# Rotary tables in rows of frequency and half with four whole stores per supertile, a new order for the first head group, and one sum for the output weights' squares

## The chip, the cores and the metric

The kernel runs on one core of a Trainium2 chip. The metric is the time of one execution on the device in microseconds (us); lower is better.

The engines are called as in the profile: PE multiplies matrices, PEld loads its stationary operand, DVE, ACT and POOL do elementwise work, and SP issues nearly all DMAs, one after the other, in the order in which the program hands them to it. "SPq" in a row is the time that SP spends on issuing one DMA. What lands later in SBUF is the transfer itself.

## The reference

Two layers of an encoder over 2048 tokens with 1024 features. Each layer normalises its input, projects it, runs eight heads of banded attention with a learned bias and four heads of retention with rotary phases beside each other, gates both, projects back and adds to its input. What the change touches is the rotary phase:

```python
def rotary_tables(positions, dim):
    inv_freq = 1.0 / (ROPE_BASE ** jnp.linspace(0.0, 1.0, dim // 2, dtype=jnp.float32))
    ang = positions.astype(jnp.float32)[:, None] * inv_freq[None, :]
    return jnp.cos(ang), jnp.sin(ang)

def apply_rotary(t, cos, sin):
    t1, t2 = jnp.split(t, 2, axis=-1)
    return jnp.concatenate([t1 * c - t2 * s, t1 * s + t2 * c], axis=-1)

def hybrid_layer(x, norm_gain, w_in, w_out, rel_bias, cos, sin):
    proj = rms_norm(x, norm_gain) @ w_in
    aq, ak, av, ag, rq, rk, rv, rg = jnp.split(proj, cuts, axis=-1)
    ya = chunked_rel_attention(aq, ak, av, rel_bias)
    yr = chunkwise_retention(rq, rk, rv, cos, sin)
    return x + jnp.concatenate([ya * silu(ag), yr * silu(rg)], -1) @ w_out
```

## The kernel before, in words

**Tiles and stages.** The tokens are cut into 4 supertiles of 512, the heads of a layer into 4 groups of two attention heads and one retention head. For a layer l, a group s and a supertile n the kernel computes: `dense_T` (from L590), four projections transposed (q, k of attention, then q, k of retention, tiles `dT`, matmuls in L763, or in quarters per token tile in L745 for the very first); `dense_V` (from L775), values and gates for the four token tiles of the supertile (tiles `dV`, L783). Each is 24 matmuls of 128x512, since every operand is split into an upper and a lower fp16 part (`hTh`, `hTl` of the input, `whT`, `wlT` of the weights) and three products are taken. The `dT` and `dV` tiles share two PSUM buffers in turn, so a tile starts only when the one before last has been read out.

**Attention and retention** of the supertile are then woven into the dense work of the next one, unit by unit. A unit of attention (its name holds group, supertile, token tile a, head: `pT_0_1_3_0` is group 0, supertile 1, a = 3, head 0) is: scores `S` on PE (L831, L832), `sc` on DVE (L835), exponential `sc` and its upper part `pq` on ACT (L838, L840), the lower part on POOL (L841), a DMA transpose to `pT` issued by SP (L843), and `o` on PE (L853, L854), which waits for `pT`. Retention (L888 on) needs q and k turned by the rotary tables: ACT reads `dT` out (L695), SP loads the halves exchanged (`swp`, L699, L700), POOL multiplies and adds ("the turn", L703 to L705), ACT and DVE split the result (L708, L711, L714), and SP transposes the keys (`kt`, L718). `swp` has one buffer, so the second `swp` of a supertile waits for the first turn.

**The tables.** `tables()` (L83) works out cosine and sine of position times frequency for one or two supertiles with DVE steps (L94 to L107), two Sin on ACT (L118, L119) and a negating copy (L121), stores them to DRAM (`tab`, L127 to L130), and `dense_T` loads them back as `tabc`, `tabs` (L646, L647) for every supertile. ACT's exponential and its Sin need different tables, and each exchange shows as an ACT_TABLE_LOAD. Three generators run: for supertile 0 (one letter `t` in the lists below is one step of it), for 1 and 2 together (`u`) and for 3 (`v`).

**Token tiles.** The input of group 0 is normalised on the fly, token tile by token tile, in steps named by the lists: `xsq` squares (ACT, L256), `xrs` the inverse root (DVE, POOL L219), `xmul` the scaling (DVE, L263), then for tokens 0 to 3 `xtr` transposes on PE (L272) and for 4 to 15 `xdma` DMA transposes (SP, L243 upper, L244 lower) after `xhi` (ACT, L278) and `xlo` (DVE, L286). `W` and `V` steps scale the weight sections of the group (`hi` on ACT L1412, `lo` on DVE L1415).

**What sets the order.** On PE, DVE, ACT and POOL the order is always the program's. In group 0 of layer 0 it is written by hand: the string given to `do()` (L1449) up to the first values, then the table `listed` (L1454), whose pairs of lists are done in turn as the attention units of supertiles 0 to 3 go by. SP keeps program order until the values of supertile 0 are done; from there the framework places most SP instructions by when their data comes, and only those marked keep their program order. `later(k, ...)` puts a store off by k turns of these lists.

**Output weights.** `prep_Omax` (L505) finds the scale of the output weights of a layer from the sum of their squares, 8 sections of 128 rows, adding section by section on DVE.

## Time and profile before

| | us |
|---|---|
| median of 3 runs | 2036.86 |
| lowest and highest of them | 2033.1, 2038.18 |
| profiled execution, its own time | 2034.96 |
| its span in the trace | 2033.0 |
| PE busy in it | 1988.2 (98%) |
| DVE, ACT, POOL busy | 1241.9, 1154.5, 705.8 |

The profiled execution lies 1.9 us below the median, and its time is 2.0 us above its span. PE is busy for nearly all of the span, so a gain must come out of PE's idle time or out of the stretches in which its clock is not at full speed. In the rows of the timelines each line gives start, duration, engine, line and operation, the tiles written and read, a count, and in brackets the idle time of the engine just before with what ended it. The windows' rows give length, then for PE, PEld, DVE, ACT and POOL the busy time with the instructions started, then PE's granted clock, the DMA engines' busy share and GB/s.

### The profile page before, as it was taken

To read this page: it belongs to the slowest core of one execution; us is meant where nothing else is said; L and a number is where in the kernel's file an instruction comes from. 1 tells how busy PE (TensorE), PEld (TensorE's weight loads), DVE (VectorE), ACT (ScalarE), POOL (GpSimd) and SP (SyncE) were. 2 spreads that over 40 slices of the span, in tenths; PEclk is the share of its full clock that TensorE was granted. 3 is DMA by queue.
4 is the path that set the end of the run, shared out by engine and by line. 5 is a ranking of instruction groups with operands and counts; after the bars stand their busy time and mean duration, and the time that the engine had idled before them with its cause. 6 is when DMAs were issued, how large, how long until landed. Compare 5 with 4: busy or idle time off the path is not lost.

```text
span 2033.0 us, 36844 instructions
## 1 busy us (share of the span) xinstructions
PE 1988.2 (98%) x12918; PEld 1046.3 (51%) x12918; DVE 1241.9 (61%) x3676; ACT 1154.5 (57%) x2526; POOL 705.8 (35%) x701
## 2 busy tenths in 40 slices
PE   7998999999999999999999999999999999999998
PEld 5444555555555555554444555555555555555544
DVE  7787766665656655676554556565655566557543
ACT  7566756466666655555445556555656565455432
POOL 1444443443344434420003444344434443443100
PEclk9999999999999999999999999999999999999999
DMA  8788775456585754899874547554656665558874
GB/s 232 184 179 163 171 141 128 104 131 140 124 183 123 164 125 104 175 226 268 220 184 101 120 104 164 113 123 104 161 119 146 160 157 133 120 116 188 229 203 135
DMA packets 645690, 313.47 MB, mean 154 GB/s; under 512 B 459232, under 2 KB 602080, under 8 KB 645504
## 3 DMA queue, kind: packets, MB, share of 16 engines
q1 hardware_dynamic: 645504, 311.12, 66.1%
q8 instruction: 101, 1.65, 0.3%
q14 instruction: 85, 0.70, 0.1%
HBM read 123.26 MB, written 41.98 MB: 81 GB/s over the span
## 4 chain that ended last, share of the span: by engine, by line
PE 86%; DMA 4%; DVE 3%; ACT 2%; POOL 2%; issue 2%; SPq 1%; POOLq 0%; ACTq 0%; DVEq 0%
PE dT L763 29%; PE dV L783 27%; PE dO L1161 15%; PE r L888 4%; PE o L853 3%; PE S L832 3%; PE S L831 3%; DMA pT<-pq 2%; PE o L854 2%; POOL swp L704 0%; PE dT L745 0%; DVE sc L835 0%; DMA xa<-in_x_dram 0%; DMA swp<-rot 0%; ACT stO0m L320 0%
## 5 line engine op out<-in xcount | busy, mean ns | idle before, releaser
L841 POOL TENSOR_TENSOR pq<-sc,pq 128x640 f16<-128x640 f32 (+4 forms) x256 | 322.8, 1261 | 958.0 <-ACT pq L840 497.4
L838 ACT ACTIVATE sc<-sc,mq,cT 128x640 f32<-128x640 f32 (+4 forms) x256 | 218.3, 853 | 416.0 <-DVE mq L837 294.2
L783 PE MATMUL dV<-whV,hTh 128*128 128x512 f16 x1024 | 352.1, 380 | 1.1 <-DVE gt L801 1.1
L783 PE MATMUL dV<-wlV,hTh 128*128 128x512 f16 x1024 | 352.2, 380 | 0.0
L783 PE MATMUL dV<-whV,hTl 128*128 128x512 f16 x1024 | 352.0, 379 | 0.0
L763 PE MATMUL dT<-hTh,whT 128*128 128x512 f16 x1008 | 348.3, 381 | 3.1 <-DMA hTh<-hTl 3.1
L763 PE MATMUL dT<-hTh,wlT 128*128 128x512 f16 x1008 | 348.1, 381 | 0.0
L763 PE MATMUL dT<-hTl,whT 128*128 128x512 f16 x1008 | 346.6, 379 | 0.0
L783 PEld LDWEIGHTS <-hTh 128*128 128x128 f16 x2048 | 196.3, 98 | 214.8 <-DVE gt L801 2.6
L763 PEld LDWEIGHTS <-whT 128*128 128x128 f16 x2016 | 192.4, 98 | 209.3 <-DVE xb L98 3.6
L835 DVE CUSTOM_DVE_ANT_0 sc<-S,bias 128x640 f32<-128x640 f32 (+4 forms) x256 | 188.4, 736 | 129.9 <-PE S L832 128.0
L1161 PE MATMUL dO<-whO,yhy 128*128 128x512 f16 x504 | 191.0, 379 | 1.1 <-DMA yhy<-hTh 1.1
L1161 PE MATMUL dO<-whO,yly 128*128 128x512 f16 x504 | 191.0, 379 | 0.3 <-DMA yly<-hTh 0.3
L1161 PE MATMUL dO<-wlO,yhy 128*128 128x512 f16 x504 | 191.0, 379 | 0.0
L840 ACT ACTIVATE pq<-sc 128x640 f16<-128x640 f32 (+4 forms) x256 | 171.5, 670 | 8.1
L1161 PEld LDWEIGHTS <-yhy 128*128 128x128 f16 x1008 | 98.1, 98 | 113.8 <-DMA yhy<-hTh 1.6
L783 PEld LDWEIGHTS <-hTl 128*128 128x128 f16 x1024 | 99.1, 98 | 110.5 <-issue 0.8
L763 PEld LDWEIGHTS <-wlT 128*128 128x128 f16 x1008 | 97.7, 98 | 109.1 <-issue 2.1
L853 PE MATMUL o<-v,pT 128*128 128x129 f16 x1120 | 132.9, 222 | 15.0 <-DMA pT<-pq 15.0
L831 PE MATMUL S<-k,q 128*128 128x128 f16 (+3 forms) x592 | 142.8, 268 | 0.0
L832 PE MATMUL S<-k,q 128*128 128x128 f16 (+3 forms) x592 | 130.0, 268 | 0.0
L853 PEld LDWEIGHTS <-pT 128*128 128x128 f16 x1120 | 103.4, 97 | 50.0 <-DMA pT<-pq 21.5
(360 smaller groups left out, 3295.4 us busy)
## 6 DMA issues: line engine op xcount, KB each, us to landing
q<-qq SPq DMA_DIRECT2D x128, 128.0 KB, 2.4
yyy<-y_d SPq DMA_DIRECT2D x32, 512.0 KB, 4.6
stT<-in_w_in_dram SPq DMA_DIRECT2D x27, 512.0 KB, 4.9
stV<-in_w_in_dram SPq DMA_DIRECT2D x26, 512.0 KB, 4.6
k<-kk SPq DMA_DIRECT2D x128, 64.0 KB, 2.0
swp<-rot SPq DMA_DIRECT2D x64, 128.0 KB, 3.1
tabc<-tab SPq DMA_DIRECT2D x32, 256.0 KB, 3.0
tabs<-tab SPq DMA_DIRECT2D x32, 256.0 KB, 3.1
```

The lines of the kernel that those rows point to most:

```text
L763: pe.matmul(ps, w_[:, j, kt, :], h_[:, kt, :], start=(m == 0), stop=(m == 23))
L783: pe.matmul(ps, h_[:, kt, a * P:(a + 1) * P], w_[:, kt, :], start=(m == 0), stop=(m == 23))
L831: pe.matmul(o, st.q[:, hx, 0, cs], k_, start=True, stop=False)
L832: pe.matmul(o, st.q[:, hx, 1, cs], k_, start=False, stop=True)
L835: dve.tensor_tensor_reduce(out=v, in0=S[:, 0:w], in1=g.bias[hx][:, 640 - w:640], scale=1.0, scalar=-3.0e38, op0=ALU.add, op1=ALU.max, accu ...
L838: act.activation(v, v, AF.Exp, bias=m[:, 0:1], scale=g.c[:, 0:1])
L840: act.activation(pq[:, 0:w], v, AF.Copy)
L841: pool.tensor_tensor(pq[:, w:2 * w], v, pq[:, 0:w], op=ALU.subtract)
L853: pe.matmul(o[:, u.hx, 0:129], u.p[:, b, :], v_, start=(b == 0), stop=False)
L854: pe.matmul(o[:, u.hx, 0:65], u.p[:, u.nb + b, :], v_[:, 0:65], start=False, stop=(b == u.nb - 1))
L888: pe.matmul(out_, w_, m_, start=(i == 0), stop=(i + 1 == len(pairs)))
L1161: pe.matmul(ps, h_[:, kt, :], w_[:, kt, :], start=(m == 0), stop=(m == 23))
```

## The change

1. **Tables.** Row p of the working tile is now frequency p/2 and half p%2 of the supertile's 512 tokens (before: half p/64, frequency p%64). So the positions of a supertile come in one DMA of 128x256 (before: two of 64x256), a part of the tables is stored by one DMA of 128x256 (before: two of 64x256), and a supertile's tables take 4 stores instead of 8. The second supertile of a pair stores all four at the 7th turn (before: four at the 7th, four at the 11th).
2. **Output weights' squares.** Each section's sum goes into a column of one tile of 128x8, and one DVE reduction sums them.
3. **The lists of group 0** are new.

```diff
-            for hf in range(2):
-                o = n * 512 + hf * 256
-                sp.dma_start(pi[hf * 64:(hf + 1) * 64, i * 256:(i + 1) * 256], pos[None, o:o + 256].to_broadcast([64, 256]))
+            src = pos[n * 512:(n + 1) * 512].rearrange("(h c) -> h c", h=2)[None].to_broadcast([64, 2, 256])
+            sp.dma_start(pi[:, i * 256:(i + 1) * 256], src)
...
-        def store(i, n, hf):
-            sl = slice(hf * 64, hf * 64 + 64)
-            cs = slice(hf * 256, hf * 256 + 256)
-            ws = slice(i * 256, i * 256 + 256)
-            sp.dma_start(tab_d[n][0, 0:64, cs], k2[sl, ws])
-            sp.dma_start(tab_d[n][0, 64:128, cs], k2[sl, ws])
-            sp.dma_start(tab_d[n][1, 0:64, cs], ang[sl, ws])
-            sp.dma_start(tab_d[n][1, 64:128, cs], r[sl, ws])
-            if hf == 1:
-                tab_done.add(n)
-
-        for hf in range(2):
-            store(0, ns[0], hf)
-            if len(ns) > 1:
-                later(7 + 4 * hf, lambda hf=hf: store(1, ns[1], hf))
+        def store(i, n):
+            for part, src in enumerate((k2, k2, ang, r)):
+                rows = tab_d[n][part // 2, part % 2 * 64:part % 2 * 64 + 64].rearrange("f (h c) -> (f h) c", h=2)
+                sp.dma_start(rows, src[:, i * 256:(i + 1) * 256])
+            tab_done.add(n)
+
+        store(0, ns[0])
+        if len(ns) > 1:
+            later(7, lambda: store(1, ns[1]))
...
-        mm = b2.tile([P, 1], F32, tag="omax", name=f"omax{nm}")
+        mm = b2.tile([P, KT], F32, tag="omax", name=f"omax{nm}")
...
-            m1 = sumsq(sts[j], f"{nm}m{j}", None)
+            act.activation(sts[j][0][0], sts[j][0][0], AF.Square, accum_out=mm[:, j:j + 1])
...
-            if j == 0:
-                dve.tensor_copy(mm, m1)
-            else:
-                dve.tensor_scalar(mm, mm, 1.0, m1[:, 0:1], op0=ALU.mult, op1=ALU.add)
-        mm = lowp(mm, nm)
-        for _ in range(5):
+        yield
+        m1 = b2.tile([P, 1], F32, tag="m1", name=f"m1{nm}", bufs=4)
+        dve.tensor_reduce(m1, mm, axis=AX.X, op=ALU.add)
+        mm = lowp(m1, nm)
+        for _ in range(4):
...
-    sp.dma_start(invf_sb, invf)
+    sp.dma_start(invf_sb, invf[0:64, None, :].to_broadcast([64, 2, 1]))
...
-    do("xsq0 g g Wsq0 xrs0 Wlp0 xsq1 g Wsc0 t Whi0 xmul0 t xtr0 xrs1 Wlo0 xmul1 xsq2 xhi0 xrs2 Wsq1 xlo0 xtr1 xsq3 "
+    do("g xsq0 xrs0 Wsq0 xsq1 g Wlp0 g Wsc0 xmul0 Whi0 xtr0 xsq2 t xrs1 xhi0 xmul1 Wsq1 Wlo0 xrs2 t xtr1 xlo0 t Wlp1 "
```

What the lists move shows best in the order of the instructions. In the changed kernel all line numbers from `tables` on are smaller, by 1 at its top and by 7 or 8 in most of the rest: the stores are L125 there, the positions L89, the token transposes L236 and L237, `swp` L691 and L692, the tables' loads L638 and L639, `pT` L835.

**First place: SP when the first tables are stored.** Before, the second half of the eight stores (the first four read alike), then four loads of positions for supertiles 1 and 2, then the first `swp` and the tables' loads:

```order
L127 DMA tab_137<-wk_169 64x256
L128 DMA tab_137<-wk_169 64x256
L129 DMA tab_137<-wk_166 64x256
L130 DMA tab_137<-wk_168 64x256
L90 DMA xb<-in_pos_dram 64x256 x4
L699 DMA swp_0_0_2_725<-rot_0_0_2_723 64x512
L700 DMA swp_0_0_2_725<-rot_0_0_2_723 64x512
L646 DMA tabc_0_0_321<-tab_137 128x512
L647 DMA tabs_0_0_322<-tab_137 128x512
L593 DMA bias_0_796<-toep_0_626 128x640
L243 DMA_TRANSPOSE hTh_1_148<-hTh_2_152 128x8x128
```

In the changed kernel, the same place:

```order
L125 DMA tab_137<-wk_169 128x256 x2
L125 DMA tab_137<-wk_166 128x256
L125 DMA tab_137<-wk_168 128x256
L691 DMA swp_0_0_2_734<-rot_0_0_2_732 64x512
L692 DMA swp_0_0_2_734<-rot_0_0_2_732 64x512
L638 DMA tabc_0_0_315<-tab_137 128x512
L639 DMA tabs_0_0_316<-tab_137 128x512
L585 DMA bias_0_798<-toep_0_643 128x640
L236 DMA_TRANSPOSE hTh_1_148<-hTh_2_152 128x8x128
```

Four stores are gone, and the positions have moved some ten places up, ahead of the first supertile's q and k. 

**Second place: ACT and POOL while the first values are computed.** `L278` (`L271` after) with `hTl_2_153` is the upper part of a token tile, here of token 7, the last that supertile 1 needs; the `dV_0_0_j` rows read out the four tiles of values of supertile 0. ACT before:

```order
L278 ACTIVATE hTl_2_153<-hTl_3_151 128x1024
L599 ACTIVATE bias_0_796<-bias_0_796,ciT_0_677 128x640
L791 ACTIVATE v_0_0_783<-dV_0_0_2_887 128x2x64
L792 ACTIVATE gt_0_0_2_921<-dV_0_0_2_887,ughV_0_740 128x256
L793 ACTIVATE rv_0_0_2_920<-dV_0_0_2_887,urvV_0_738 128x128
L794 ACTIVATE rv_0_0_2_920<-rv_0_0_2_920 128x128
L708 ACTIVATE rot_0_0_2_723<-rot_0_0_2_723 128x512
L791 ACTIVATE v_0_0_783<-dV_0_0_3_932 128x2x64
```

ACT in the changed kernel:

```order
L591 ACTIVATE bias_1_846<-bias_1_846,ciT_0_604 128x640
L783 ACTIVATE v_0_0_776<-dV_0_0_2_883 128x2x64
L784 ACTIVATE gt_0_0_2_914<-dV_0_0_2_883,ughV_0_690 128x256
L785 ACTIVATE rv_0_0_2_913<-dV_0_0_2_883,urvV_0_688 128x128
L786 ACTIVATE rv_0_0_2_913<-rv_0_0_2_913 128x128
L271 ACTIVATE hTl_2_153<-hTl_3_151 128x1024
L700 ACTIVATE rot_0_0_2_732<-rot_0_0_2_732 128x512
L783 ACTIVATE v_0_0_776<-dV_0_0_3_931 128x2x64
```

Token 7's upper part now stands behind the third read-out, and both biases ahead of it. POOL before, from the inverse roots (`rsn`) of tokens 6, 5 and 7 on:

```order
L219 TENSOR_TENSOR rsn_6_799<-ssn_6_706,mhalf 128x1
L219 TENSOR_TENSOR rsn_5_803<-ssn_5_752,mhalf 128x1
L219 TENSOR_TENSOR rsn_7_818<-ssn_7_653,mhalf 128x1
L703 TENSOR_TENSOR rot_0_0_2_723<-rot_0_0_2_723,tabc_0_0_321 128x512
L704 TENSOR_TENSOR swp_0_0_2_725<-swp_0_0_2_725,tabs_0_0_322 128x512
L705 TENSOR_TENSOR rot_0_0_2_723<-rot_0_0_2_723,swp_0_0_2_725 128x512
L597 MEMSET bias_0_796 64x64
```

POOL in the changed kernel:

```order
L212 TENSOR_TENSOR rsn_5_790<-ssn_5_720,mhalf 128x1
L212 TENSOR_TENSOR rsn_6_794<-ssn_6_713,mhalf 128x1
L695 TENSOR_TENSOR rot_0_0_2_732<-rot_0_0_2_732,tabc_0_0_315 128x512
L696 TENSOR_TENSOR swp_0_0_2_734<-swp_0_0_2_734,tabs_0_0_316 128x512
L697 TENSOR_TENSOR rot_0_0_2_732<-rot_0_0_2_732,swp_0_0_2_734 128x512
L589 MEMSET bias_0_798 64x64
L590 MEMSET bias_0_798 64x64
L212 TENSOR_TENSOR rsn_7_849<-ssn_7_675,mhalf 128x1
```

Token 7's inverse root has moved from ahead of the turn to behind it, and with it the DVE steps that use it (`xmul7`, `xlo6`), which now stand ahead of DVE's read-out of the second value tile, `dV_0_0_1`.

**Third place: SP at the end of supertile 1's attention.** Before (three of supertile 3's stores, `tab_140`, and token 15's upper transpose stand ahead of these rows; the `DMA_TRANSPOSE` of `hTl_3_151` is the lower part of token 15):

```order
L244 DMA_TRANSPOSE hTl_3_151<-xa 128x8x128
L127 DMA tab_140<-xb 64x256
L128 DMA tab_140<-xb 64x256
L843 DMA_TRANSPOSE pT_0_1_3_0_2186<-pq_0_1_3_0_2183 128x10x128
L130 DMA tab_140<-xb 64x256
L129 DMA tab_140<-xb 64x256 x2
L943 DMA y_d_111<-yr_0_6_2240 128x128
L305 DMA stT_12_2455<-in_w_in_dram 128x8x128
L163 DMA gb_5174<-in_gain_dram 128x1024
L843 DMA_TRANSPOSE pT_0_1_3_1_2270<-pq_0_1_3_1_2267 128x10x128
L718 DMA_TRANSPOSE kt_0_2_2308<-rot_0_2_3_1938 128x8x128
```

In the changed kernel:

```order
L298 DMA stT_11_2325<-in_w_in_dram 128x8x128
L835 DMA_TRANSPOSE pT_0_1_3_0_2163<-pq_0_1_3_0_2160 128x10x128
L125 DMA tab_140<-xb 128x256 x4
L237 DMA_TRANSPOSE hTl_3_151<-xa 128x8x128
L935 DMA y_d_111<-yr_0_6_2221 128x128
L298 DMA stT_12_2450<-in_w_in_dram 128x8x128
L710 DMA_TRANSPOSE kt_0_2_2288<-rot_0_2_3_1924 128x8x128
L835 DMA_TRANSPOSE pT_0_1_3_1_2254<-pq_0_1_3_1_2251 128x10x128
```

The lower part of token 15 (`L237`) now stands behind `pT_0_1_3_0` and the stores. `pT_0_1_3_0` has moved ahead of all the stores of supertile 3's tables, and `kt` ahead of `pT_0_1_3_1`. On ACT the Sin of these tables with its table load has moved from ahead of the exponential of unit `0_1_3_0` to between it and that of `0_1_3_1`.

More of the change, by code (lines that the diff above doesn't have):

```diff
@@ L1447, in do @@
             steps[nm]()
-    do("xsq0 g g Wsq0 xrs0 Wlp0 xsq1 g Wsc0 t Whi0 xmul0 t xtr0 xrs1 Wlo0 xmul1 xsq2 xhi0 xrs2 Wsq1 xlo0 xtr1 xsq3 "
[3 rows of a table removed]
+    do("g xsq0 xrs0 Wsq0 xsq1 g Wlp0 g Wsc0 xmul0 Whi0 xtr0 xsq2 t xrs1 xhi0 xmul1 Wsq1 Wlo0 xrs2 t xtr1 xlo0 t Wlp1 "
[3 rows of a table added]
     g00.vdone = 4
-    listed = iter([("bt xrs6 xhi4 xrs5", "xmul6 xlo4 xdma4"), ("xrs7 xmul5", ""), ("xhi5", "xmul7 xlo5"), ("", "xhi6 x8"),
[16 rows of a table removed]
+    listed = iter([("xrs5 u xrs6 xmul5 xhi4 bt", "xhi5 xmul6 xlo5"), ("", "xlo4"), ("xdma5", ""), ("bt", "bt xrs7 xhi6"),
[16 rows of a table added]
     att = [None]
```

38 rows, old and new, of tables (listed, steps) are left out of this document.

## The prediction

> **What bounds the kernel now.** PE does. I first cut the span by the windows view, at the places where PE stops; each row gives length, PE's busy time with its count, then PEld, DVE, ACT, POOL, and PE's granted clock.
>
> ```profile
> 0.00:45.02 45.02, 30.37 (x298) 23.32 (x298) 34.84 (x103) 35.32 (x66) 4.77 (x18) 1.00 0.86 250
> ...
> 65.63:77.22 11.59, 8.50 (x29) 3.24 (x27) 8.26 (x13) 3.89 (x9) 4.67 (x6) 0.71 0.77 209
> ...
> 108.33:120.30 11.97, 8.15 (x55) 4.17 (x55) 10.91 (x21) 6.55 (x18) 7.94 (x7) 0.96 0.77 189
> ...
> 164.00:197.15 33.15, 26.34 (x174) 13.54 (x171) 21.34 (x62) 22.12 (x48) 14.24 (x10) 0.95 0.99 199
> 197.15:2033.00 1835.85, 1819.46 (x11817) 954.72 (x11814) 1091.02 (x3312) 1026.65 (x2264) 635.25 (x623) 1.00 0.65 150
> ```
>
> After 197 us PE lacks 16.4 us in 1836, and the new lists end about there. So the change can win only in the first 197 us, and the steady part is cover for anything small that it adds. What PE waits for, summed over the span:
>
> ```profile
> PE o L853 <- DMA pT<-pq: 15.0, 9, 3.1
> ...
> PE dT L763 <- DMA hTh<-hTl: 3.1, 1, 3.1
> ...
> PE dV L783 <- DVE gt L801: 1.1, 2, 0.5
> ```
>
> The timeline of PE shows where these fall and what follows a pause:
>
> ```profile
> 65.52 0.38 PE L783 MATMUL dV<-wlV,hTh 128*128 128x512 f16 x1
> 68.99 3.57 PE L763 MATMUL dT<-hTh,whT 128*128 128x512 f16 x8 [3.09 <-DMA hTh<-hTl]
> ...
> 72.57 3.08 PE L763 MATMUL dT<-hTh,wlT 128*128 128x512 f16 x8
> 75.49 1.89 PE L763 MATMUL dT<-hTl,whT 128*128 128x512 f16 x8
> ...
> 109.72 0.23 PE L853 MATMUL o<-v,pT 128*128 128x129 f16 x1 [1.39 <-DMA pT<-pq]
> ...
> 118.87 0.23 PE L853 MATMUL o<-v,pT 128*128 128x129 f16 x1 [2.43 <-DMA pT<-pq]
> ...
> 119.78 0.63 PE L783 MATMUL dV<-wlV,hTh 128*128 128x512 f16 x1
> ...
> 184.79 0.29 PE L853 MATMUL o<-v,pT 128*128 128x129 f16 x1 [3.12 <-DMA pT<-pq]
> ...
> 194.26 0.23 PE L853 MATMUL o<-v,pT 128*128 128x129 f16 x1 [1.63 <-DMA pT<-pq]
> ```
>
> I call these gaps A (68.99), B (109.72), C (118.87), E (184.79), F (194.26). After A the same eight matmuls take 3.57 and 3.08 before they take 1.89: the clock is low for a while (0.71 in that window). So A costs 3.3 of waiting and about 2.8 of slow matmuls (1.64 + 1.19 over the full-speed spacing), 6.1 in all. After C eight large matmuls run at 0.63 in place of 0.38, some 0.21 apart more: 2.4 + 1.7 = 4.1. E likewise costs about 4.5, its slow stretch being shorter. B (1.39) and F (1.63) have no slow stretch. With two smaller pauses of 2.1 together these sum to near 20 us.
>
> [...]
>
> **Part 1, the tables.** SP's own rows, at the first tables and at the places that make A and C late:
>
> ```profile
> 42.08 0.55 SPq L127 DMA_DIRECT2D tab<-wk  x1
> ...
> 46.52 0.59 SPq L130 DMA_DIRECT2D tab<-wk  x1
> 47.16 2.51 SPq L90 DMA_DIRECT2D xb<-in_pos_dram  x4
> ...
> 51.63 0.44 SPq L647 DMA_DIRECT2D tabs<-tab  x1
> ...
> 61.50 0.48 SPq L699 DMA_DIRECT2D swp<-raw  x1
> ...
> 65.63 1.27 SPq L243 DMA_TRANSPOSE hTh<-hTl  x1
> ...
> 108.01 0.58 SPq L127 DMA_DIRECT2D tab<-xb  x1
> ...
> 111.19 2.20 SPq L1230 DMA_DIRECT2D xin<-in_x_dram  x2
> 113.50 1.22 SPq L843 DMA_TRANSPOSE pT<-pq  x1
> ```
>
> A store of 64 rows costs SP 0.55 to 0.60, and a load of 128 rows (`tabs`) 0.44. A store of 128 rows does not occur, so I bound it: 0.44 below; above, two of the old ones, 1.2. I take 0.6, since all plain DMAs lie near that, whatever their rows. The 16 stores and 4 position loads that vanish are then 20 x 0.6 = 12 us of SP, but SP's time counts only where something urgent is queued behind.
>
> [...]
>
> **Part 2, the first 45 us: +1.0.** In the new lists DVE does more table arithmetic before it gives the first group's second weight section its scale and its lower part:
>
> ```profile
> 26.39 0.41 DVE L94 SCALAR_TENSOR_TENSOR wk<-wk,wk 128x256 f32<-128x256 f32 x1
> ...
> 27.59 0.42 DVE L107 SCALAR_TENSOR_TENSOR wk<-wk,wk 128x256 f32<-128x256 f32 x1
> 28.04 0.29 DVE L97 TENSOR_SCALAR wk<-wk 128x256 f32<-128x256 f32 x1
> ```
>
> Two of the first kind (0.8) stand ahead of the scale; and one, the second kind and two roundings (0.41 + 0.42 + 0.58 = 1.4) ahead of the lower part. PE's projections wait for both, but it has other token tiles to fill with, and `xmul1` goes ahead of the first section's lower part (1.28), which feeds PE sooner. Bounds: -1.3 if that gain carries through, +2 if all 1.4 and a slip of ACT's reach PE. I take +1.0, near the 0.8 and 1.4. The values of supertile 0 then start at 46.0 in place of 45.02 and, at 20.61/4 = 5.15 each, the fourth at 61.5 and the end at 66.7.
>
> **Part 3, gap A: from 6.1 to 1.8.** Before, token 7's upper transpose was issued at 65.63 because two transposes and `swp` stood ahead, and `swp` waited at 61.50 for the first turn on POOL to free its buffer:
>
> ```profile
> 50.93 1.46 POOL L219 TENSOR_TENSOR rsn<-ssn,mhalf 128x1 f32<-128x1 f32 x1 [2.27 <-DVE ssn L217]
> 55.10 1.98 POOL L703 TENSOR_TENSOR rot<-rot,tabc 128x512 f32<-128x512 f32 x1 [2.71 <-ACT hTl L278]
> ...
> 59.37 1.33 POOL L705 TENSOR_TENSOR rot<-rot,swp 128x512 f32<-128x512 f32 x1
> ...
> tabs<-tab SPq DMA_DIRECT2D x32, 256.0 KB, 3.1
> ...
> tab<-wk SPq DMA_DIRECT2D x8, 64.0 KB, 2.1
> ```
>
> Now the stores (43.9 to 46.3, since the Sin come some 1.8 later behind the values' weights) must land (2.1 to 3) before `tabc` can be read, so the tables arrive at about 49.5 + 3.1 = 52.6. The turn takes 60.7 - 55.1 = 5.6 and ends at 58.3, `swp` is free then, and token 7's transpose waits only for its upper part, which ACT writes behind the third read-out (62.7) at 63.75; issue 63.8, landing 3.3 later as before (65.63 to 68.99), at 67.1. Against PE's 66.7 that is a gap of 0.4.
>
> But POOL's inverse root for token 7 now stands behind the turn: two memsets (0.6) and it (about 1.1, between its rows of 0.5 and 1.5) end at 60; DVE then does
>
> ```profile
> 53.21 0.41 DVE L801 SCALAR_TENSOR_TENSOR gt<-gt,dV 128x256 f32<-128x256 f32 x1
> 53.54 1.28 DVE L263 SCALAR_TENSOR_TENSOR hTl<-hTl,rsn,gb 128x1024 f32<-128x1024 f32 x1
> 54.74 1.22 DVE L286 TENSOR_TENSOR hTh<-hTh,hTh 128x1024 f16<-128x1024 f32 x1
> ```
>
> `xmul7`, `xlo6`, and only then the read-out of the second value tile (three steps, 0.9), until 63.3. The fourth value tile needs that buffer at 61.5, so PE stalls 1.8, and the end moves to 68.5, behind token 7's landing. A costs 1.8 (0 to 4) in place of 6.1: **-4.3**.
>
> **Part 4, supertile 1: B -1.3, C -4.0, a new one +0.8.** Ahead of B's `pT` one transpose fewer is queued (about 1.3): the gap of 1.39 goes. Ahead of C's `pT` stood four stores and a double load of 2.20; its data were ready near 107.9, and it was issued at 113.50. Now one load and one small store stand there, so it goes out at 109 or so; landing took 118.87 - 113.50 = 5.4, hence 114.5, and PE needs it at 116.4. C closes whole. On the other side, all six first stores of supertiles 1 and 2 now stand ahead of `pT_0_0_0_1` (3.6 us by 0.6 each, where five halves stood); by my count it lands within -0.5 to +1.5 of need: +0.8.
>
> **Part 5, gaps E and F: -1.** Their rows on ACT and SP:
>
> ```profile
> 173.24 1.28 ACT L838 ACT_TABLE_LOAD   x1 [0.46 <-DVE mq L837]
> ...
> 181.79 1.33 SPq L843 DMA_TRANSPOSE pT<-pq  x1
> ...
> 186.89 3.21 SPq L843 DMA_TRANSPOSE pT<-pq  x1
> ```
>
> `pT_0_1_3_0` loses the table load (1.28) and the stores ahead of it, and goes out 4 us or more sooner: E closes (4.5). But the two table loads, the Sin and the four stores now fall between it and `pT_0_1_3_1`, and so does `kt` (1.2 to 2.3). That one I get issued near 187.3 on the old clock, as late as the 186.89 of before, landing between 190.5 and 194. PE, not held by E, needs it at about 188. So most of E comes back at F, with its slow stretch. Between -3 and +2, I take **-1.0**.
>
> **The rest: 0.** The bias writes of the next group (`toep`) now stand ahead of `pT_0_2_3_1`; PE had no wait there. The output weights' sums save 7 DVE steps of about 0.15 per layer, in the steady part, where PE has 99% of the time; without that cover it would be 1 us per layer. The frequencies' load has twice the rows, once, at the very start, where the first tokens are still on their way.
>
> **Sum:** 1.0 - 4.3 - 1.3 - 4.0 + 0.8 - 1.0 = -8.8. The profiled execution took 2034.96, so 2026.2; the median lies 1.9 higher, so I say **2027.5** for it, a little under 2028.1 because two small pauses of before (2.1 together) may shrink too.
>
> **The rivals.**
>
> *The engines behind PE are the bound in supertiles 1 to 3.* PE's pauses may be what is left over when DVE, ACT, POOL and SP take their time (DVE 10.91 of 11.97 us in the window of C); then gaps closed at A to C open again further on, and only about 2 us stay: 2035. Against it: between 120 and 164 PE hardly paused.
>
> *The whole stores bring little*: they cost SP and the transfers as much as two halves. Then the tables come 2.5 us later, A stalls by 4.3, B to F stay as above: 2030 to 2032.
>
> *Slower: the tables come late and hold PE at the fourth value tile.* By Part 3 each us by which the tables land after about 51 is one us of PE, since the turn, the inverse root, `xmul7`, `xlo6` and the read-out stand in a row on POOL and DVE; and from a stall of some 2.4 on the clock falls too (2.8, as at A). The sum is eaten up when the stall is 1.8 + 8.8 - 2.8 = 7.8, that is, when the tables land at 58.6. Whole stores that took four times as long (10 us on SP's queue) would do that, to about 60, and give some 2040; for it speaks that the new pattern is not in the trace, against it that its pieces are as long as before.
>
> *More than forecast*: F closes too, and PE gains in the first 45 us: 2019.
>
> **Chances.** My forecast 0.50 (its own spread 2022 to 2033); more than forecast 0.12; the engines as bound 0.15; stores that bring little 0.07; late tables 0.16. 0.3% is 6.1 us, about what a measurement of this kernel tells from no change, so faster means under 2030.7, slower over 2043. From the forecast's case 0.40 falls to faster, 0.08 to same and 0.02, for what the first 45 us might cost, to slower; the case above it adds 0.12 to faster; the engines' 0.15 is same; the stores' 0.07 is split; late tables give 0.06 to same and 0.10 to slower. So 0.56, 0.32, 0.12. The range takes in all but the tails of the outer cases: 2017 to 2040.
>
> **What would show it.** A: the first `dT` of supertile 1 with a pause under 0.5 and no matmul of 0.63 behind it, and a `dV` that waits for `gt` by 1 to 3 us before. C: no `o` with a pause over 1 near 110 to 120. E and F: one pause in place of two, at `pT_0_1_3_1`. The first `dV` near 46.0. If PE's sum of waits for `pT` stays at 15, the first rival holds; if the first whole store takes SP over 1 us, the second or third.

## The result, and the profile after

| | before | changed |
|---|---|---|
| median of 6 runs | 2037.0 us | 2016.72 us |
| lowest, highest | 2033.1, 2038.41 | 2015.17, 2018.1 |
| profiled execution, its span | 2034.96, 2033.0 | 2016.13, 2014.4 |

The changed kernel is faster: the ratio of times is 0.9904, 95% interval 0.9892 to 0.9917, or 20 us. I had forecast 2027.5 and a range of 2017 to 2040, so the sign was right, the size was half of what came, and the time lies 0.3 us below the range.

The page and the windows of the changed kernel, cut where I had cut before (the first values, the end of supertile 0's values, the point of the program that lay at 200.4 us before):

```profile
PE 1981.2 (98%) x12918; PEld 1044.2 (52%) x12918; DVE 1230.4 (61%) x3662; ACT 1154.8 (57%) x2526; POOL 700.3 (35%) x701
```

```profile
0.00:46.09 46.09, 30.52 (x297) 22.70 (x298) 36.08 (x109) 36.76 (x71) 4.87 (x18) 1.00 0.83 253
46.09:66.79 20.70, 20.70 (x97) 9.31 (x95) 18.00 (x26) 12.69 (x25) 11.86 (x13) 1.00 1.00 206
66.79:181.70 114.91, 113.55 (x734) 59.13 (x734) 90.70 (x239) 81.05 (x172) 49.45 (x48) 1.00 0.89 194
181.70:2014.40 1832.70, 1816.41 (x11794) 953.03 (x11792) 1085.59 (x3290) 1024.26 (x2261) 634.13 (x622) 1.00 0.64 150
```

The clock is at 1.00 in every window, where it was 0.71 to 0.96 in four of them. PE's busy time is 7.0 us less for the same 12918 matmuls, for the most part since the clock is at 1.00 in every stretch of 2 us up to 2010 (in the kernel before it was at 0.50 from 68.15 to 74.98, from 119.35 to 122.77 and from 184.21 to 187.62). Behind 181.70 PE lacks 16.3 us, as before. Between 60 and 200 us all that PE waits for is this:

```profile
PE o L845 <- DMA pT<-pq: 1.0, 1, 1.0
PE dT L755 <- DVE hTl L279: 0.4, 1, 0.4
```

In the same window the kernel before waited for 10.2 us on `pT`, 3.1 on `hTh` and 0.5 on `dT`. To see where the gain is made, I took the start of PE's n-th matmul from the traces. The row "before" gives that time; every other row gives the lead over it in us. At each n of the table the first n matmuls are the same ones in all seven kernels, in part in another order. The columns stand at the first values (298), behind A (440), ahead of B (580), behind C (740), ahead of the two small pauses (900), ahead of E (1020), behind F (1100) and at the end (12900):

```
n                           298    440    580    740    900   1020   1100  12900
before, us                 45.0   81.2  105.1  136.2  159.4  178.8  196.6 2024.3
changed                    -1.1    4.5    4.8   10.7   10.9   13.4   18.7   18.6
old_tables_new_lists       -1.2    0.8    0.4   -0.9   -0.6    1.9    6.4    4.0
new_tables_old_lists       -0.6    3.9    3.4    7.5    4.3    6.1    5.2    3.2
old_0_35                   -1.3    3.4    3.4    7.7    8.0    9.1   13.2    9.3
old_36_59                  -0.6    5.0    5.3   11.1    8.6   11.0    9.6    8.0
mid_both                   -1.3    4.3    4.6   10.4   10.4    9.4   13.4   12.5
```

The changed kernel loses 1.1 us up to the first values, wins 5.6 at pause A, 5.9 at B and C, 2.5 at two small pauses (0.47 and 1.60 before) that I had left out of the sum, 5.3 at E and F, and nothing after. Each row is one execution, and behind n = 1100, where hardly anything differs between the programs, the rows still move by up to 3.9; so a few us at the end of a row say little, and times are compared by the medians. The changed kernel's timeline shows the first matmul of the values, and the two pauses that are left:

```profile
46.10 0.38 PE L775 MATMUL dV<-whV,hTh 128*128 128x512 f16 x1
...
67.39 1.89 PE L755 MATMUL dT<-hTh,whT 128*128 128x512 f16 x8 [0.40 <-DVE hTl L279]
...
175.57 0.23 PE L845 MATMUL o<-v,pT 128*128 128x129 f16 x1 [0.96 <-DMA pT<-pq]
```

SP's queue at the places of the prediction, in the changed kernel:

```profile
43.69 2.01 SPq L125 DMA_DIRECT2D tab<-wk  x4
46.56 0.47 SPq L691 DMA_DIRECT2D swp<-rot  x1
...
57.59 0.53 SPq L691 DMA_DIRECT2D swp<-raw  x1
...
64.06 1.23 SPq L236 DMA_TRANSPOSE hTh<-hTl  x1
...
102.13 1.22 SPq L835 DMA_TRANSPOSE pT<-pq  x1
...
161.50 2.98 SPq L835 DMA_TRANSPOSE pT<-pq  x1
164.57 1.98 SPq L125 DMA_DIRECT2D tab<-xb  x4
...
170.54 2.48 SPq L835 DMA_TRANSPOSE pT<-pq  x1
```

A whole store costs SP 0.50, less than one of the old halves. The first stores, the second `swp` and token 7's transpose stand within 0.7 us of where I had put them (43.9, 58.3 and 63.8). `pT_0_1_3_1` went out at 170.54; with the lead of 13.4 that is 183.9 on the old clock (186.89 before), and I had said 187.3.

### The profile page after: what moved, and what is told of

Its sections match the earlier page's. It is cut to its first block, busy times and chain, and to the rows that moved or that the text cites. A ratio compares the mean times of both kernels' runs of the same rounds, so it can differ in the third digit from the quotient of the medians.

```text
span 2014.4 us, 36802 instructions
## 1 busy us (share of the span) xinstructions
PE 1981.2 (98%) x12918; PEld 1044.2 (52%) x12918; DVE 1230.4 (61%) x3662; ACT 1154.8 (57%) x2526; POOL 700.3 (35%) x701
## 4 chain that ended last, share of the span: by engine, by line
PE 90%; DMA 3%; DVE 2%; ACT 2%; issue 1%; POOL 1%; SPq 1%; POOLq 0%; ACTq 0%; DVEq 0%
PE dT L755 31%; PE dV L775 29%; PE dO L1153 15%; PE r L880 4%; PE o L845 3%; PE S L824 3%; PE S L823 3%; DMA pT<-pq 2%; PE o L846 2%; DMA stO0m<-in_w_out_dram 1%; PE dT L737 0%; PE ptn L1026 0%; DMA rl<-in_rel_dram 0%; ACT sc L830 0%; DMA bias<-toep 0%
## 5 line engine op out<-in xcount | busy, mean ns | idle before, releaser
L846 PE MATMUL o<-v,pT 128*128 128x65 f16 x1120 | 125.7, 193 | 0.0
```

Source lines behind the costliest of these rows:

```text
L846: pe.matmul(o[:, u.hx, 0:65], u.p[:, u.nb + b, :], v_[:, 0:65], start=False, stop=(b == u.nb - 1))
```

## The experiments

My theory after the result: the gain is the pauses A to F and their slow stretches, the whole stores and the lists each being needed at different ones. The rivals were that the stores alone or the lists alone make it. Times are medians; each ratio is to the kernel before, measured beside it on the same chip, with a median of 2036.6 to 2038.8. So the kernels are compared by their ratios (0.001 is 2.0 us), the changed kernel's being 0.9904 (0.9892 to 0.9917); the timelines are of one execution each.

**1. The two parts apart.** First the changed kernel with the old `tables()` and the old frequencies' load:

```diff
-                sp.dma_start(rows, src[:, i * 256:(i + 1) * 256])
+            sp.dma_start(tab_d[n][0, 0:64, cs], k2[sl, ws])
...
+                later(7 + 4 * hf, lambda hf=hf: store(1, ns[1], hf))
```

> The changed kernel with the tables of before (rows of half and frequency, eight stores of 64 rows, two position loads per supertile); the new lists stay. Theory (both parts matter, each at its own gaps): at the first tables SP is 2.2 us longer (four more stores of 0.55), the turn on POOL starts at 53 in place of 50.8, the fourth value tile stalls by about 1, supertile 1's first transposes get later by 2; the pauses C, E, F stay closed: 2019 to 2023. Rival 1 (the whole stores make the gain): the pauses A and C come back, 2030 or more. Rival 2 (the lists make all of it): 2018 or less.

2026.89, ratio 0.995 (0.9933 to 0.9967): between theory and rival 1. The profiled execution took 2030.99, so its pauses may be larger than in the median:

```profile
69.50 3.51 PE L762 MATMUL dT<-hTh,whT 128*128 128x512 f16 x8 [2.13 <-DMA hTh<-hTl]
...
118.97 0.29 PE L852 MATMUL o<-v,pT 128*128 128x129 f16 x1 [4.40 <-DMA pT<-pq]
...
184.40 0.81 PE L762 MATMUL dT<-hTl,whT 128*128 128x512 f16 x3 [1.71 <-DMA hTl<-xa]
```

A is back with a slow stretch (3.51 for eight matmuls), C is larger than before (4.40 against 2.43), and token 15's lower part, queued behind eight stores, is late by 1.71.

Then the kernel before with the new tables alone:

> The kernel before with the new tables alone (whole stores, whole position loads), old lists. Theory: SP loses 2.2 us of stores and 1.2 us of position loads ahead of the first swp, so the turn and the second swp come about 3 us sooner and pause A mostly closes (5 of 6.1); C loses two stores (1.2) and shrinks to about 1.2 without a slow stretch (2.9); E loses 1.5 of stores at most: 2027 to 2030. Rival 1 (stores make the gain): 2020 or less. Rival 2 (lists make it): 2034 or more.

2034.95, ratio 0.9987 (0.9975 to 1.0): 2.6 us gained (0 to 5.1), and the number of rival 2. The lead table shows why so little is left: A to C give 7.5 us by n = 740, about what theory said, but 5.2 by n = 1100. Two pauses take it back, of which the first is new and the second is E, grown from 3.12:

```profile
148.68 0.23 PE L846 MATMUL o<-v,pT 128*128 128x129 f16 x1 [3.23 <-DMA pT<-pq]
...
181.07 0.23 PE L846 MATMUL o<-v,pT 128*128 128x129 f16 x1 [4.85 <-DMA pT<-pq]
```

So alone the tables give 2.6 us and the lists 10.2, together 19.6. Neither rival holds as an account: the tables' part (stores, position loads and the turn at which they are stored) is worth 9 us under the new lists and 3 under the old ones.

**2. The lists cut in two.** The string up to the first values (`do`) or the table of pairs (`listed`) taken from before, all else new:

> The changed kernel with the old table of pairs (from the first values on), the new string (up to them) and the new tables. Theory: A closes, since the tables come sooner by the whole stores; B to F come back but for the part the whole stores save: 2027 to 2031, like the new tables with old lists and 1 us more for the first 45 us. Rival (the string itself carries a gain): 2024 or less.

2033.19, ratio 0.9975 (0.9966 to 0.9984): slower than the theory's 2027 to 2031, and within the intervals as with all old lists; it has the same pauses (3.00 at 148.28, 4.83 at 180.92).

> The changed kernel with the old string up to the first values, and the new table of pairs. Theory: the gain lies in the pairs and the tables; the string costs 1.0 in the first 45 us and is not needed for A: 2015 to 2017. Rival (the string is needed so that the tables and token 7 come in time): 2020 or more, with a pause before supertile 1's first projection.

2018.73, ratio 0.9913 (0.9893 to 0.9932). By the ratio the string is worth 1.8 us, which the intervals do not tell from nothing: the gain is in the pairs and the tables.

**3. Pause A.** I lengthened SP's work at the first tables. Each first store split in two:

```diff
+                if n == 0:
+                    for o in (0, 64):
+                        sp.dma_start(rows[o:o + 64], src[o:o + 64, i * 256:(i + 1) * 256])
+                    continue
                 sp.dma_start(rows, src[:, i * 256:(i + 1) * 256])
```

> The changed kernel, with each of the four whole stores of the first supertile's tables split into two of 64 rows. Read-out theory (the turn on POOL, the inverse root of token 7, its scaling and token 6's lower part hold the read-out of the second value tile, with 1.0 us to spare in the changed kernel): SP 2.0 us longer, tables 2.0 later, a stall of 1.0 at the fourth value tile and up to 1 more at supertile 1's first projection: 2017.5 to 2019. Rival (there is no such chain; only the second swp and the transposes behind it matter): no wait of dV, and a pause of 1 to 2 at the projection. Rival 2 (all of SP's time there is hidden): 2016 to 2017, no new pause.

2021.36, ratio 0.9915 (0.9896 to 0.9935), some 2 us above the changed kernel, though the intervals overlap; the profiled execution, the slowest of four (2024.21), shows the first rival's signs:

```profile
43.36 4.94 SPq L127 DMA_DIRECT2D tab<-wk  x8
...
65.64 1.25 SPq L240 DMA_TRANSPOSE hTh<-hTl  x1
```

```profile
69.15 3.48 PE L759 MATMUL dT<-hTh,whT 128*128 128x512 f16 x8 [2.49 <-DVE xb L97]
```

Eight halves take 4.94 where four whole ones take 2.01. Token 7's transpose goes out 1.6 later (64.06 before the split) and lands at 68.90. PE waits 2.49, nearly all of it for that transpose (the row names a DVE step that ended just before 69.15), and its next eight matmuls take 3.48 in place of 1.89. The read-out of the values is not late: the turn takes 3.9 us where it took 5.1.

The first stores issued three times:

```diff
                 sp.dma_start(rows, src[:, i * 256:(i + 1) * 256])
+                if n == 0:
+                    sp.dma_start(rows, src[:, i * 256:(i + 1) * 256])
+                    sp.dma_start(rows, src[:, i * 256:(i + 1) * 256])
```

> The changed kernel, with the first supertile's four whole stores issued three times over (8 DMAs more that do no work, about 4 us of SP). Read-out theory: a stall of 3 at the fourth value tile (4 less the 1.0 to spare), slope one, with a slow stretch behind it: 2020 to 2023. Rival (only swp and the transposes): no wait of dV, a pause of 3 to 4 at the projection. Rival 2: hidden, 2017.

2034.05, ratio 0.9987 (0.9974 to 0.9999). The dose was larger than meant: as I read it, the repeated stores waited for the landing of those that they overwrite (46.69 after 46.67), and `swp` went out at 61.92 in place of 46.56. That is a strong test of the chain of Part 3:

```profile
66.13 1.26 POOL L698 TENSOR_TENSOR rot<-rot,tabc 128x512 f32<-128x512 f32 x1 [18.20 <-DMA tabc<-tab]
```

```profile
74.27 0.61 PE L778 MATMUL dV<-whV,hTh 128*128 128x512 f16 x1 [12.51 <-DVE gt L796]
```

The fourth value tile waited 12.51 for the read-out, exactly where the prediction's slower rival put it, for tables that came 15.4 later, and the time comes close to that of the kernel before.

**4. Pause C.** The stores of supertiles 1 and 2 split in the same way:

> The changed kernel, with the whole stores of supertiles 1 and 2 split into two of 64 rows (8 DMAs more; 6 of them ahead of the second pT, two later). Theory (pauses come from what is queued ahead of one pT): a pause of 0 to 2.5 at the first units of supertile 1, C stays closed since the split stores are all issued long before it: 2016 to 2019. Rival (C comes back with the number of stores, as with the old tables): 2021 to 2025, with a pause over 3 and a slow stretch near 115.

2023.57, ratio 0.9924 (0.9905 to 0.9943), 4 us above the changed kernel: the rival. SP's rows and PE's pause:

```profile
107.25 1.91 SPq L1226 DMA_DIRECT2D xin<-in_x_dram  x2
109.28 1.21 SPq L839 DMA_TRANSPOSE pT<-pq  x1
```

```profile
115.10 0.29 PE L849 MATMUL o<-v,pT 128*128 128x129 f16 x1 [3.31 <-DMA pT<-pq]
```

The stores are over by 100.5, but SP is then behind, and the framework, which places SP's instructions by when their data come, puts two transposes of a token and two loads of 512 KB ahead of the `pT` whose data POOL had ready at 104.0. From then to its issue that `pT` waits 5.30 us here, 5.85 with the old tables, 5.57 in the kernel before, 2.39 with the new tables under the old lists, where C is gone too, and 0.13 in the changed kernel. So C is this wait on SP, and, as I read it, it hangs on how full SP is in the 15 us before, not on what the lists put next to `pT`.

**5. Pauses E and F.** First I moved Sin and stores back:

```diff
-("xdma13 xhi15", ""), ("", "xlo14 v"), ("", "v"), ("v v", "xlo15")
+("xdma13 xhi15", "v v v v"), ("", "xlo14"), ("", ""), ("", "xlo15")
```

> The changed kernel, with the last steps of supertile 3's tables (lower clip, magnitude, Sin, copy) moved three pairs up in the list, so that the Sin and its table load stand on ACT ahead of the exponential of unit 0_1_3_0, and the four stores on SP ahead of its pT, as before the change. Theory 1 (E came mainly from that place): pT_0_1_3_0 is late by 2 or more, a pause of 2 to 4 near 168 and a slow stretch: 2019 to 2022. Theory 2 (E came from DVE and SP running behind PE, which the rest of the new order has ended): pT_0_1_3_0 goes out 1.5 to 2 later within its slack, and the pause of 0.96 at 175.6 shrinks: 2015 to 2018.

2015.88, ratio 0.989 (0.9871 to 0.9908): theory 2's number. The place of the Sin and of the stores, on which my Part 5 was built, costs nothing that shows in the new order. Its trace is not quite theory 2's: F is gone, but unit `0_1_3_0` now pauses for 1.18 and the one ahead of it for 0.66. Then the pairs by thirds, each taken from before:

> The changed kernel, with the pairs of the list that fall into the middle of group 0 (supertile 3's tables, tokens 12 to 15) taken from before; all else new. Theory (E and F were closed by where these steps now stand): DVE and SP fall behind PE again, pauses of 3 or more near 148 or near 175 come back with a slow stretch, the lead over the kernel before falls from 17 at the end of the group to 12 or less: 2021 to 2025. Rival (the lead that the earlier pairs give is enough, E and F close by themselves): 2015 to 2018.

2028.26, ratio 0.9947 (0.9928 to 0.9965): more is lost than the theory's range said.

> The changed kernel, with the first pairs of the list (tokens 4 to 11, the tables of supertiles 1 and 2, the biases) taken from before; all else new. Theory (they close A to C together with the whole stores): a pause of 1 to 2 at A, 0.5 to 1 at B, C closed by the whole stores, the lead at 110 us about 4 in place of 7, and E, F still closed by the later pairs: 2019 to 2023. Rival (the pauses made early are given back by E and F anyway): 2015 to 2018.

2024.26, ratio 0.9924 (0.9902 to 0.9946); pauses of 1.31 at A, 0.80 at B, none at C, then 1.17 at 166 and 2.23 at 181, where theory had E and F closed. The first pairs are worth 4 us, not all of it at their own place.

> The changed kernel, with the last pairs of the list (the next group's weights) taken from before; all else new. Theory (PE hardly pauses there in either kernel): 2015 to 2018. Rival (some of the gain comes from these pairs): 2019 or more, the lead falling between 200 and 300 us.

2019.2, ratio 0.9903 (0.9882 to 0.9924), the changed kernel's own: no effect, though the median alone is the rival's.

The middle pairs carry 8.8 us, the largest part. The timelines of PE and DVE with the old middle pairs show what is late:

```profile
144.37 0.23 PE L845 MATMUL o<-v,pT 128*128 128x129 f16 x1 [2.55 <-DMA pT<-pq]
...
175.95 0.29 PE L845 MATMUL o<-v,pT 128*128 128x129 f16 x1 [4.29 <-DMA pT<-pq]
```

```profile
157.67 1.22 DVE L231 TENSOR_TENSOR xa<-xin,xa 128x1024 f16<-128x1024 f32 x1
158.80 2.42 DVE L1232 SCALAR_TENSOR_TENSOR xin<-xin,rsn,gb 128x1024 f32<-128x1024 f32 x1
...
162.14 0.81 DVE L827 CUSTOM_DVE_ANT_0 sc<-S,bias 128x640 f32<-128x640 f32 x1
```

The scores of unit `0_1_3_0` were ready at about 158.5, and DVE read them at 162.14, behind the lower part of token 14 and the scaling of token 15. The kernel before has the same rows (scores ready at about 169.5), and the changed kernel does not:

```profile
167.63 1.22 DVE L238 TENSOR_TENSOR xa<-xin,xa 128x1024 f16<-128x1024 f32 x1
168.77 2.42 DVE L1240 SCALAR_TENSOR_TENSOR xin<-xin,rsn,gb 128x1024 f32<-128x1024 f32 x1
...
172.10 0.81 DVE L835 CUSTOM_DVE_ANT_0 sc<-S,bias 128x640 f32<-128x640 f32 x1
```

```profile
156.31 0.82 DVE L827 CUSTOM_DVE_ANT_0 sc<-S,bias 128x640 f32<-128x640 f32 x1 [0.62 <-PE S L824]
```

In the changed kernel DVE waits for the scores, not they for it. Six kernels ask whether these two steps are the cause. (Where they are taken out of the way, token 14's DMA transposes, `xdma14`, come three pairs later with them, since they need its lower part; in before_tokens_apart SP then issues two lower transposes shortly ahead of `pT_0_1_3_0` where it had one.) Put back alone, put back with the Sin and the stores, and taken out of the kernel before:

```diff
-("", "xmul15 v"), ("v", ""), ("xdma13 xhi15", ""), ("", "xlo14 v")
+("", "v"), ("v xlo14", "xmul15"), ("xdma13 xhi15", ""), ("", "v")
```

> The changed kernel, with the scaling of token 15 and the lower part of token 14 put back on DVE ahead of the score step of unit 0_1_3_0 (as before the change); Sin and stores stay behind. DVE theory: the score step starts 2.5 to 3.7 late, since these two long steps (1.2 and 1.3 to 2.4) run when its scores are ready, pT_0_1_3_0 goes out as much later, and E comes back with 1 to 3 us of pause: 2018 to 2021. Rival (E is a matter of SP's queue and the DMAs): no change, 2015 to 2018.

2019.32, ratio 0.9904 (0.9888 to 0.9921): by the ratio no effect, as the rival said, though the median alone lies in the theory's range. E does not come back; the one pause left, F, grows from 0.96 to 1.90.

> The changed kernel, with both put back ahead of unit 0_1_3_0: the two long DVE steps (scaling of token 15, lower part of token 14) and the Sin with its table load and the four stores. Sum theory (each alone fits into the slack of some 3 us that pT_0_1_3_0 has there, together, 2.5 to 3.7 on DVE, 1.3 on ACT and 2 on SP, they don't): E is back with 2 to 4 us and a slow stretch, 2020 to 2024. Rival (neither matters in the new order): 2015 to 2019.

2019.91, ratio 0.9909 (0.9893 to 0.9926), which no measurement here tells from the changed kernel: the sum theory's price falls. What came is not E but retention waiting for DVE, so that `pT_0_1_3_0` had landed when PE came to it (it landed 12.95 after its scores, so against the 11.9 at which PE is otherwise free some 1 us of E would have come):

```profile
169.46 0.29 PE L880 MATMUL r<-rv,dT 128*128 128x128 f16 x1 [1.89 <-DVE dT L888]
```

> The kernel before, with only these two DVE steps moved: the scaling of token 15 one pair up, the lower part of token 14 two pairs down. DVE theory: pause E (3.12 and its slow stretch) shrinks below 1.5 while the Sin stays where it was; F stays: 2032 to 2035 beside 2037. Rival (SP's stores hold pT_0_1_3_0 anyway): E stays over 2.5, 2036 to 2038.

2035.89, ratio 0.9985 (0.9974 to 0.9997), 3 us gained (0.6 to 5.3). E fell from 3.12 to 1.16, which looks like the DVE theory. But a pause of 1.60 has opened at 178.11, at the unit ahead, `0_1_2_1`, where the kernel before has none; so PE waits 2.76 in place of 3.12, and what is saved is mostly E's slow stretch. F is at 1.90 (1.63 before).

> The kernel before, with both taken out of the way of unit 0_1_3_0 (the two DVE steps, and Sin with its load behind it, as in the change), its eight stores and kt now ahead of pT_0_1_3_1. Theory of the prediction (what E gives comes back at F): E under 0.5, F grows from 1.63 to 3 to 5 with a slow stretch: 2034 to 2037 beside 2037. Rival (F does not grow, since its unit's whole chain comes sooner): E under 0.5 and F under 2: 2029 to 2033.

2033.79, ratio 0.9974 (0.9962 to 0.9986): 5.3 us gained (2.9 to 7.7), of which the profiled execution shows 1.8 by the end of F. E is gone, the pause of 1.61 at `0_1_2_1` is there too, and F is this:

```profile
191.58 0.29 PE L853 MATMUL o<-v,pT 128*128 128x129 f16 x1 [2.35 <-DMA pT<-pq]
```

F grew by 0.7 and got a slow stretch (a clock of 0.50 in 191.58 to 193.58), so a part of E does come back there, but far less than the prediction had it. Last, the old middle pairs mended, first by token 12's lower transpose moved behind `pT_0_1_1_0` (`xdma12` seven pairs later), then also by the two DVE steps:

> The changed kernel with the middle pairs of before (which paused 2.55 at 144.4 and 4.29 at 176), and in them token 12's lower transpose moved behind pT_0_1_1_0. SP theory: that pT is issued 1.4 sooner behind one transpose less and meets less traffic, and the pause near 144 falls below 1.2; E stays: 2025 to 2027 beside 2028. Rival (the pause comes from the 512 KB load ahead of it): it stays over 2.

2028.17, ratio 0.9949 (0.9934 to 0.9964): no effect on the time; the pause is 1.85 where it was 2.55, between theory and rival, and E is at 4.58.

> The changed kernel with the middle pairs of before, token 12's lower transpose behind pT_0_1_1_0, and the two DVE steps (scaling of token 15, lower part of token 14) out of the way of unit 0_1_3_0. If both theories hold: pauses under 1.2 near 144 and under 2 near 170 to 180, most of the 11 us between the middle pairs of before and after: 2018 to 2021. If only the SP theory: 2025 to 2027; if neither: 2028.

2022.41, ratio 0.9915 (0.99 to 0.993): 6.5 of the 8.8 us of the middle pairs. E's 4.58 and its slow stretch have become pauses of 1.80 and 2.23 at 165 and 175, at units `0_1_2_1` and `0_1_3_0`, and neither drew a slow stretch (the clock is at 1.00 from 160 to 182). Behind the second is ACT: with the score step out of DVE's way, its exponential waits for the Sin, the upper part of token 15 and the table load back:

```profile
159.19 1.28 ACT L117 ACT_TABLE_LOAD   x1
...
162.55 1.28 ACT L830 ACT_TABLE_LOAD   x1
163.85 0.92 ACT L830 ACTIVATE sc<-sc,mq,cT 128x640 f32<-128x640 f32 x1
```

The traces tell what all these kernels have in common, if one follows unit `0_1_3_0` from the end of its scores on PE. The columns give, in us: how long the score step waits to start on DVE; from its start to that of the exponential on ACT; from the end of POOL's lower part to the issue of `pT` on SP; from there to its landing; then the landing, and the moment at which PE was free for it, both counted from the end of the scores; and PE's pause.

```
                        DVE    ACT     SP   landing   landed  PE free  pause
before                 2.53   2.44   4.08      2.95    15.17    12.10   3.12
changed                0.04   1.17   0.72      5.46    10.69    11.85   0.00
sin_ahead              2.90   2.44   0.48      5.70    14.68    13.55   1.18
late_tokens            2.40   1.16   0.03      3.67    10.43    11.86   0.00
sin_and_tokens         4.37   2.44   0.03      2.95    12.95    16.53   0.00
before_tokens_apart    0.65   3.97   3.99      3.13    14.91    13.79   1.16
before_tokens_and_sin  1.71   1.16   0.03      5.32    13.21    13.64   0.00
old_36_59              3.61   2.44   2.53      5.63    17.37    13.13   4.29
mid_both               1.56   3.98   2.62      4.84    16.17    13.99   2.23
```

PE is free some 11.9 us after the scores, later where it paused in between, and the pause is what the landing exceeds that by. Between the kernel before and the changed one the path loses 2.5 us of waiting on DVE, 1.3 on ACT (the table load) and 3.4 on SP, and its landing takes 2.5 longer. So E is not the work of one step. Taking the two token steps out (before_tokens_apart) makes the score step 1.9 sooner, but ACT then holds the unit 1.5 longer and SP as long as before, and it lands only 0.3 sooner after its scores; putting them back (late_tokens) costs 2.4 on DVE, and a quicker issue and landing make up for it.

The data of `pT_0_1_3_0` are POOL's lower part; these are its rows before and after, and SP issues at 181.79 and 161.50:

```profile
176.31 1.40 POOL L841 TENSOR_TENSOR pq<-sc,pq 128x640 f16<-128x640 f32 x1 [0.50 <-ACT pq L840]
```

```profile
159.25 1.53 POOL L833 TENSOR_TENSOR pq<-sc,pq 128x640 f16<-128x640 f32 x1 [0.82 <-ACT pq L832]
```

**6. The output weights' squares.** The old way of adding them, all else new:

> The changed kernel, with the squares of the output weights added section by section as before. Theory: 8 small DVE steps per layer more, beside a PE that is busy: 2015 to 2018, no new pause. Rival: these steps stand ahead of a read-out that PE waits for: 2019 or more.

2017.51, ratio 0.9897 (0.9876 to 0.9918): no effect. The profiled execution, the slowest of four (2022.0), has pauses of 1.22 at 163 and 2.12 at 178, so F is not small in every execution of the new order.

## Why the prediction was wrong

That pauses A to F would close through SP's queue and the new order was right, but in Part 5, the largest miss, the step to F was wrong, and Parts 3 and 4 were mis-sized. The parts forecast 8.8 us and the trace shows 18.6; of the 9.8 between them Part 5 makes 4.3, the two small pauses 2.5, Part 4 1.4 and Part 3 1.3.

- **Part 1, a whole store costs 0.6:** right, 0.50. Four whole stores take SP 2.01 (changed kernel), and the eight halves that hold the same data 4.94 (split_first).
- **Part 2, +1.0 up to the first values:** right; they start at 46.10, I had said 46.0, and with the old string at 44.66 (old_do_new_listed). Which of its steps make this was not tried.
- **Part 3, A from 6.1 to 1.8:** too small a gain by 1.3 (5.6 in place of 4.3). The stall that I feared at the fourth value tile did not come. POOL began the turn at 50.78, when `tabc` had landed, and I had let it wait until 52.6; token 7's inverse root took 0.62 where I had 1.1; so the read-out ended at 60.56, and the tile needed it at 61.56. The chain itself is real (12.51 in triple_first), with 1.0 us to spare, and the second swp has even less (split_first).

```profile
50.78 1.54 POOL L695 TENSOR_TENSOR rot<-rot,tabc 128x512 f32<-128x512 f32 x1 [2.79 <-DMA tabc<-tab]
...
56.41 0.62 POOL L212 TENSOR_TENSOR rsn<-ssn,mhalf 128x1 f32<-128x1 f32 x1
```

- **Part 4, B and C closed (5.3 together), a new pause of 0.8:** the first is right (5.9); the second did not come.
- **Part 5, E and F together -1.0: this step failed.** They gave 5.3, and the two small pauses ahead of them, which I had only mentioned, 2.5. That E would close by the table load and the stores was right as far as it went (1.3 on ACT and 3.4 on SP, by the table of experiment 5). What failed is the step that `pT_0_1_3_1` is issued "near 187.3 on the old clock" and that "most of E comes back at F". I had worked this out by keeping ACT, DVE and POOL at the times that they had before, and let only PE move. The runs show 183.9 in its place and a pause of 0.96. `pT_0_1_3_0` had gone out 6.9 sooner on the old clock (161.50 + 13.4 against 181.79), where I had "4 us or more": I had not priced the two long token steps (1.22 and 2.42) that stand ahead of its score step on DVE and that the change moves (2.5). Behind it, the score step of `0_1_3_1` waits 2.13 where it waited 3.63, its `pT` waits on SP for 1.53 where it waited 3.00, and it lands in 4.99 where it took 7.33. The change's third place with the two DVE steps, made alone in the kernel before, gives 5.3 (before_tokens_and_sin), and there F grows to 2.35, so a part of my step is real under the old order and the eight stores. What stays open is which of the other middle pairs shorten the path in the new order; no run takes them one by one.
- **The first rival** (gaps closed early come back further on) is what happens to the new tables under the old lists: 7.5 us won by the end of C, 5.2 left behind F and 3.2 at the end. I had given it 0.15 as the fate of the whole change, and had not asked which part of the change would prevent it: the middle pairs do.
- **The range and the chances:** the lower end, 2017, is what my own first part gives when all of the near 20 us go and nothing is lost (2034.96 - 20 + 1.9 = 2016.9). Nearly that came, to which the nearest of my cases, "more than forecast", gave 0.12: the pauses gave 19.3, the first 45 us lost 1.1, and the profiled execution took 2016.13. That the median lies only 0.6 above it, and not 1.9 as before, is why 2016.72 still lies under 2017.

## What to carry to other kernels

When a stall in a pipeline goes, do not work out the next stage on the old clock: look up whether each engine behind was waiting for the one that was stalled, or was late by itself, and let the waiting ones move with it. A step list is priced by what each long step runs into: a step of 1.2 us that needs nobody may sit right ahead of the one that everybody needs. Price a wait by its whole path: add up what one unit waits on each engine, on the queue and for the landing, and set the sum against the time until it is needed; moving one step helps only as far as the next wait on that path lets it. And where two parts of a change feed the same queue, ask for the gain of each alone and of both: here 3, 10 and 20 us.

## What the runs showed of the hardware

**After which pauses the clock fell.** Over all 20 profiles, looking at pauses of PE over 1.2 us between 60 and 230 us: with the 19 pauses of 1.85 us or less the granted clock stayed at 1.00; of the 18 from 1.89 to 3.23, 10 drew a clock of 0.50, for 3.41 us each (6.83 at A of the kernel before), at A and E of that kernel from 0.8 and 0.6 before PE went on; all 9 from 3.31 up drew it. So a pause of 1.89 (sin_and_tokens) can cost 3.6, by my estimate of half of 3.41 on top of it, and whether it does is not a matter of its length alone (2.35 drew it, 3.23 did not). The prediction had the clock fall from a stall of some 2.4 on, as at C (2.43); 1.89 and 2.13 (old_tables_new_lists) drew it too, and 3.00 (new_do_old_listed) did not.

**A DVE step beside a busy POOL, and beside an idle one.** The long step that held up the scores took 2.42 us in the kernel before (168.77, above), where POOL was at work beside it, its own lower part of 128x640 taking 2.24 there and 1.40 at 176.31; the same form of DVE step took 1.28 where POOL was idle, in the changed kernel. The rows of the kernel before, and then that one:

```profile
167.87 2.24 POOL L841 TENSOR_TENSOR pq<-sc,pq 128x640 f16<-128x640 f32 x1 [2.16 <-ACT pq L840]
170.07 2.26 POOL L703 TENSOR_TENSOR raw<-raw,tabc 128x512 f32<-128x512 f32 x1
```

```profile
137.97 1.28 DVE L1232 SCALAR_TENSOR_TENSOR xin<-xin,rsn,gb 128x1024 f32<-128x1024 f32 x1
```

POOL's turn took 5.1 us while DVE was at work (changed kernel, 50.78 to 55.87) and 3.8 while it was idle (triple_first, 66.13 to 69.95). In the kernel before, DVE's step began 1.34 us ahead of the end of POOL's (167.87 + 2.24 = 170.11) and ended 1.08 behind it; what made either of them longer no row shows. So a step's price in one place of the order is not its price in another.
